# Moving three visits of the scores in the first layer, and splitting three norm sums into fp32r halves, in a two-layer decoder step

## The chip, the cores and the metric

The kernel runs on one core of one Trainium2 chip. The metric is the time of one execution in microseconds of device time; the time before is the median of three runs. The engines are named as in the profile: PE (TensorE, its weight loads shown apart as PEld), DVE (VectorE), ACT (ScalarE), POOL (GpSimd) and SP (SyncE, which issues nearly all DMAs). A profile is one further execution, taken by the hardware profiler.

## What is computed

One inference step of a decoder with two layers, for a prompt of 256 positions and for 8 samples of one position each. All 264 columns share the weights. Cut to what matters here:

```python
def rmsnorm(x, g):
    y = xf * lax.rsqrt(jnp.mean(xf * xf, axis=-1, keepdims=True) + EPS)
    return (y * g).astype(x.dtype)

# layer 0: block-sparse attention (A) beside a gated MLP (B)
q, k, v, bu, bv = jnp.split(rmsnorm(x, norm_g) @ w_in, ...)
a = moba_attention(rope(q), rope(k), v)          # softmax over causal scores
bvn = layer_norm(gelu(bv), sgu_gain)
b_out = gelu(bu) * (tril(sgu_w) @ bvn + sgu_b)
x = x + concat(a, b_out) @ w_out
# ConvFFN of each layer
h = rmsnorm(x, norm_g)
g = h @ w_gate
gc = sum(conv_w[i] * g_all[:, i:i + T] for i in range(CONV_W)) + conv_b
x = x + (gelu(gc) * (h @ w_up)) @ w_down
# layer 1: stick-breaking attention beside causal pooling, then a second ConvFFN
```

The model width is 1024, the ConvFFN's 2816, there are 8 heads of 64 in A. Everything is float32. The outputs are the new activations (after a final norm) and the new cache rows and states.

## The kernel before

Activations lie transposed: 128 features on the partitions, 264 columns (256 prompt, 8 samples) along the free axis, so the width of 1024 is 8 tiles.

**Weights and products.** The weights of all phases stream through in one order, as blocks of 128x128. Eight blocks are a tile. For each tile ACT rounds the raw weights to fp32r (wh, line 299) and DVE subtracts to get the rest (wl, line 300). An activation operand is kept as two halves as well, and a block is three PE products of 264 columns (high by high, high by low, low by high) that add into one PSUM bank; all of PE's matmuls have line 215. `split` prepares tiles three ahead; four buffers each for wh and wl mean that tile t+4 can be rounded when PE is done with tile t. The projection's outputs take turns in four PSUM banks (pool "mm"); four other banks (pool "at") serve attention and norms. Other line numbers below are those of the instruction's call.

**The phases** are in0 (160 blocks: bv, q, k, bu, v), out0 (64), ff0 and dn0 (the ConvFFN's gate and up projections, and its down projection), then in1, out1, ff1, dn1.

**Order by hand.** In in0, out0, in1 and out1 PE's instructions stay in the order in which the program gives them. Other work is hung into this order by hooks: `blk(b, f)` calls f after b blocks of the phase. SP's loads are kept in order too (`late`). All else, and PE in the ConvFFNs, is ordered by the compiler's list scheduler, which simulates the engines; DVE, ACT and POOL then run their queues in order.

**The first layer's hooks that matter here.** In in0, four visits `s_qk(t)` compute the causal scores of heads 2t and 2t+1: two mask products, eight products of q by k (S), then in `s_soft` four maxima on DVE (lines 703, 704), four exponentials on ACT (706, 707), reciprocals (708) and scalings (709 on DVE, 710 on ACT). Visit t needs q's and k's tile t with their rotation, done by `in0_evac` in four DVE steps (shuffle 670, products 672 or 674 and 675, sum 676); k's tile t is complete after block 72 + 8t. `s_tr` transposes the probabilities of one head (pt). `gm_mean` at block 100 adds bv's four tiles in three DVE steps (bsum, lines 785 to 787), the first of which is kept behind the DVE step given just before it; `gm_var` at block 108 has PE sum them over the partitions (pmu).

**The norms.** `residual` builds, for each of the 8 output tiles of out0, dn0, out1 and dn1, the new X (DVE, line 581), the next operand's halves (ACT 384, DVE 385), and a square (ACT 397) that POOL adds to an accumulator (409). `Norm.finish` calls `rstd_of`, which sums over the partitions by a PE product with a matrix of ones in fp32 (ns; each such product shows as two PE instructions), and makes R = 1/rms in two ACT steps (421, 422). The norm ahead of the first ConvFFN is f0, that ahead of layer 1 is n1, that ahead of the second ConvFFN f1; the first (n0) and the last (fin) add a second part. After f0 and f1, `gelu_set` loads another activation table behind R (517), and the evacuation of each gate tile multiplies by R (wk, line 552), followed by the convolution (553 to 556), gelu (558), the product with the up tile (563) and the split of the result (a_h 432, a_l 433). `norm1` calls finish for n1 at block 12 of in1, where PE's order is kept.

Of the kernel before, what the change touches and what calls it, by code (L numbers as in the profile page):

```python
# [9 lines left out]
F32 = mybir.dt.float32  # L10
F32R = mybir.dt.float32r
BF16 = mybir.dt.bfloat16
I32 = mybir.dt.int32
AF = mybir.ActivationFunctionType
ALU = mybir.AluOpType
# [3 lines left out]
P = 128  # L19
D = 1024  # L20
# [3 lines left out]
T = SEQ + NS  # L24
# [178 lines left out]
def tile_decoder_step(ctx: ExitStack, tc: tile.TileContext, a):  # L203
    nc = tc.nc
    v, s, g = nc.vector, nc.scalar, nc.gpsimd
# [14 lines left out]
    pe = TensorE()  # L220

    con = ctx.enter_context(tc.tile_pool(name="con", bufs=1))
# [4 lines left out]
    sm = ctx.enter_context(tc.tile_pool(name="sm", bufs=3))  # L227
# [27 lines left out]
    def vec(n):  # L255
        o, w = _VEC[n]
        return VEC[:, o:o + w]
# [117 lines left out]
    ident = cst("ident")  # L375
    ones = con.tile([P, P], F32, name="ones")
    v.memset(ones, 1.0)
    epst = con.tile([P, 1], F32, name="epst")
    v.memset(epst, EPS)

# [9 lines left out]
    class Norm:  # L390
# [17 lines left out]
            else:  # L408
                g.tensor_tensor(self.acc, self.acc, q, ALU.add)

        def finish(self, pin=False):
            return rstd_of([self.acc] + self.last, 1.0 / D, self.name, pin)

    def rstd_of(parts, scale, name, pin=False, bank=None):
        p = (bank or at)(f"ns_{name}")
        for i, x in enumerate(parts):
            mm = pe.matmul(p[:, :T], ones, x, start=i == 0, stop=i == len(parts) - 1)
            if pin:
                tc.keep_in_program_order(mm)
        R = sm.tile([P, T], F32, tag="R", name=f"R_{name}", bufs=2)  # L420
        s.activation(R, p[:, :T], AF.Ln, bias=epst, scale=scale)
        last[0] = s.activation(R, R, AF.Exp, scale=-0.5)
        return R

# [91 lines left out]
    def gelu_set():  # L516
        tc.keep_in_program_order(s.preload_act_table_set("gelu_apprx_tanh_and_others"))

    def sigmoid_set():
        tc.keep_in_program_order(s.preload_act_table_set("sigmoid_and_others"))  # L520
# [17 lines left out]

    def ffn(l, xg, R, down_evac, hooks=None):
        cw, cb = vec("cw"), vec("cb")  # L540
        wc = lambda i, j: cw[:, (l * 3 + i) * NF + j:(l * 3 + i) * NF + j + 1]
        cvo = sm.tile([P, NF, 10], F32, tag="cvo", name=f"cvo{l}", bufs=1)
        act = [mv(f"a{l}_{i}") for i in range((NF + 3) // 4)]
        half = {}

        def evac(m, o):
            n, j = m
            if n == "g":
                wk = f4(f"wk{l}_{j}", (P, 2, T))
                C = wk[:, 0, :]  # L550
                G = wk[:, 1, :]
                v.tensor_tensor(G, o, R, ALU.mult)  # L552
                s.activation(C, G, AF.Identity, scale=wc(2, j), bias=cb[:, l * NF + j:l * NF + j + 1])
                v.scalar_tensor_tensor(C[:, 1:SEQ], G[:, 0:SEQ - 1], wc(1, j), C[:, 1:SEQ], ALU.mult, ALU.add)
                v.scalar_tensor_tensor(C[:, 2:SEQ], G[:, 0:SEQ - 2], wc(0, j), C[:, 2:SEQ], ALU.mult, ALU.add)
                v.tensor_tensor(C[:, SEQ:T], C[:, SEQ:T], C0[:, l, j, :], ALU.add)
                s.activation(cvo[:, j, :], G[:, SEQ - 2:T], AF.Copy)
                s.activation(C, C, AF.Gelu_apprx_tanh)
                half[j] = wk
            else:  # L560
                wk = half.pop(j)
                C, A = wk[:, 0, :], wk[:, 1, :]
                v.tensor_tensor(A, o, C, ALU.mult)
                halves(*hl(act, j), A)

        run(orders[f"ff{l}"], lambda m, k: hl(xg, k), evac)
        nc.sync.dma_start(a[f"cv{l}"], cvo)
        lnexp()
        run(orders[f"dn{l}"], lambda m, k: hl(act, k), down_evac, hooks)

    def residual(gain, name, operand=True, R=None):
        xg = [mv(f"xg_{name}{i}") for i in range(2)] if operand else None
        nrm = Norm(name, not operand)

        def evac(m, o):
            m = m[1]
            if R is not None:
                z = sm.tile([P, T], F32, tag="rz", name=f"z_{name}{m}", bufs=4)
                v.tensor_tensor(z, o, R, ALU.mult)
                o = z  # L580
            v.tensor_tensor(X[:, m, :], X[:, m, :], o, ALU.add)
            if operand:
                operand_tile(xg[m // 4], m, X[:, m, :], gain[:, m:m + 1])
            nrm.add(m)
            if not operand:
                s.activation(X[:, m, :], X[:, m, :], AF.Copy, scale=gain[:, m:m + 1])
        return xg, nrm, evac
# [9 lines left out]
    nrm = Norm("n0", True)  # L597
# [212 lines left out]
    def gm_norm():  # L810
        Rb = rstd_of([st0["acc"]], 1.0 / 512, "sgu", bank=mmb)
        for t in range(4):
            v.scalar_tensor_tensor(bv4[:, t, :], bv4[:, t, :], vec("sg")[:, t:t + 1], Rb, ALU.mult, ALU.mult)
        bvn = sm.tile([P, 4, NS], F32, tag="bvn", name="bvn", bufs=1)
        g.tensor_copy(bvn, bv4[:, :, SEQ:T])
        nc.sync.dma_start(a["bvn"], bvn)
        st0["vgt"] = f4("vgt", (P, 2, 512))
# [45 lines left out]
    blk(40, masks)  # L863
    blk(44, gm_first)
    blk(72, sm_q)
    for t, b in enumerate((82, 95, 108, 121)):
        blk(b, s_qk, t)
    for t, b in enumerate((103, 116, 129, 142)):
        blk(b, s_tr, 2 * t)
        blk(b, s_tr, 2 * t + 1)  # L870
    blk(96, sgu_load)
# [33 lines left out]
    xg, nrm, evac = residual(vec("f0"), "f0")  # L905
    run(orders["out0"], pick([catA, catB]), evac, hk)
    fixed[0] = False
    R = nrm.finish()
    gelu_set()
    xg1, nrm1, evac = residual(vec("n1"), "n1", R=R)  # L910
    ktiles, kload = page_list(a["kt1"], "K1")
# [19 lines left out]

    def norm1():
        nonlocal R
        R = nrm1.finish()
        sigmoid_set()

    edge = f4("edge", (P, 384))
# [117 lines left out]
    fixed[0] = True  # L1055
    blk = lambda b, f, *x: hk.at(b / 8 - 1, f, *x)
    blk(12, norm1)
    blk(33, pool_sum)
    for n in range(8):
# [25 lines left out]
    xg, nrm, evac = residual(vec("f1"), "f1")  # L1085
    run(orders["out1"], pick([catA, catB]), evac, hk)
    fixed[0] = False
    R = nrm.finish()
    gelu_set()
    _, nrm, evac = residual(vec("fin"), "fin", operand=False, R=R)  # L1090
    ffn(1, xg, R, evac)
    R = nrm.finish()
    for i, (m, e) in enumerate(YD):
        x = X[:, m:e, :]
# [71 lines left out]
```

## Time and profile before

| what | value |
|---|---|
| median of 3 runs | 603.81 us (603.23 to 604.2) |
| the profiled execution | 605.38 us, span 603.6 us |
| mean granted PE clock | 0.997 |
| PE busy | 590.4 us in 4900 matmuls |
| DVE busy | 424.7 us in 745 instructions |
| ACT busy | 339.9 us in 597 |
| POOL busy | 42.8 us in 59 |
| read from and written to memory | 117.65 MB and 3.96 MB |

A row of a timeline gives an instruction's start and its duration in us, then engine, line, operation, output and inputs, and in brackets how long the engine had been idle before and what released it. A row of the chain gives start, length and what held the chain. Matmuls overlap in the pipeline, so a PE instruction's shown duration is longer than its share of the stream. A row of waits reads: who waited, for whom, us in total, how often, longest.

### The profile page before, as it was taken

The numbers are of one execution on the slowest core, as the hardware profiler recorded it, in microseconds if no ns is written. First come the engines' busy times: TensorE is split into PE (matmuls) and PEld (weight loads), VectorE is DVE, ScalarE is ACT, GpSimd is POOL, SyncE is SP. The second block draws the span as 40 slices with busy tenths as digits, with TensorE's granted clock in tenths as the row PEclk, the third lists the DMA queues.
The fourth block names the chain that finished last, engine by engine and source line by source line (L and its number), as shares of the span: only waits on it lengthen the run. The fifth ranks groups of instructions, "written<-read, shape, count | busy, mean of one in ns | idle before, by whom it ended". The sixth has DMA issues, their size and how long they took to land.

```text
span 603.6 us, 12258 instructions
## 1 busy us (share of the span) xinstructions
PE 590.4 (98%) x4900; PEld 571.4 (95%) x4900; DVE 424.7 (70%) x745; ACT 339.9 (56%) x597; POOL 42.8 (7%) x59
## 2 busy tenths in 40 slices
PE   8989999999999999999999999999999999999994
PEld 7988879999999999999999878999999999999993
DVE  6899565958878778576569676686877777755542
ACT  7557754656555656454454466656665555555431
POOL 4101002300000000001120000030000000001210
PEclk9999999999999999999999999999999999999998
DMA  8998845454554645796466763554545545455402
GB/s 310 352 378 328 272 153 205 155 204 149 201 176 174 208 150 201 260 370 212 151 251 248 262 206 113 173 205 148 208 149 201 179 171 207 152 208 171 179 1 72
DMA packets 28090, 122.39 MB, mean 203 GB/s; under 512 B 3330, under 2 KB 5250, under 8 KB 16642
## 3 DMA queue, kind: packets, MB, share of 16 engines
q1 hardware_dynamic: 27200, 120.42, 56.4%
q10 hardware_dynamic: 834, 1.20, 0.6%
q8 instruction: 38, 0.62, 0.4%
q14 instruction: 18, 0.15, 0.1%
HBM read 117.65 MB, written 3.96 MB: 201 GB/s over the span
## 4 chain that ended last, share of the span: by engine, by line
PE 91%; DVE 2%; DMA 2%; SPq 2%; ACT 2%; issue 1%; ACTq 0%; DVEq 0%
PE mm L215 83%; DMA raw<-in_w 1%; PE pv_l L215 1%; PE sc L215 1%; SPq L340 1%; PE pav L215 1%; PE pt L218 1%; DVE wl L300 1%; DMA PT<-in_pt 1%; ACT wh L299 1%; PE S L215 1%; PE Z L215 1%; SPq L274 0%; PE pf L215 0%; DVE X L1095 0%
## 5 line engine op out<-in xcount | busy, mean ns | idle before, releaser
L299 ACT ACTIVATE wh<-raw 128x1024 fp32r<-128x1024 f32 x179 | 189.6, 1062 | 198.6 <-PE mm L215 185.1
L300 DVE TENSOR_TENSOR wl<-raw,wh 128x1024 fp32r<-128x1024 f32 x179 | 219.1, 1225 | 112.5 <-ACT wh L299 111.5
L215 PE MATMUL mm<-xg_f_h,wh 128*128 128x264 f32 x704 | 200.6, 285 | 0.3 <-DVE wk L552 0.3
L215 PE MATMUL mm<-xg_f_l,wh 128*128 128x264 f32 x704 | 199.9, 284 | 0.0
L215 PE MATMUL mm<-xg_f_h,wl 128*128 128x264 f32 x704 | 198.6, 282 | 0.0
L215 PEld LDWEIGHTS mm<-xg_f_h,wh 128*128 128x128 f32 x704 | 132.2, 188 | 0.8 <-issue 0.7
L215 PEld LDWEIGHTS mm<-xg_f_l,wh 128*128 128x128 f32 x704 | 132.3, 188 | 0.1
L215 PEld LDWEIGHTS mm<-xg_f_h,wl 128*128 128x128 f32 x704 | 132.2, 188 | 0.0
L215 PE MATMUL mm<-a_h,wh 128*128 128x264 f32 x352 | 99.9, 284 | 0.0
L215 PE MATMUL mm<-a_l,wh 128*128 128x264 f32 x352 | 99.8, 284 | 0.0
L215 PE MATMUL mm<-a_h,wl 128*128 128x264 f32 x352 | 99.3, 282 | 0.0
L215 PEld LDWEIGHTS mm<-a_l,wh 128*128 128x128 f32 x352 | 66.1, 188 | 0.0
L215 PEld LDWEIGHTS mm<-a_h,wh 128*128 128x128 f32 x352 | 66.1, 188 | 0.0
L215 PEld LDWEIGHTS mm<-a_h,wl 128*128 128x128 f32 x352 | 66.1, 188 | 0.0
L215 PE MATMUL mm<-xg_h,wh 128*128 128x264 f32 x160 | 48.2, 302 | 1.1 <-ACT xg_h L384 1.1
L215 PE MATMUL mm<-xg_l,wh 128*128 128x264 f32 x160 | 46.2, 289 | 0.0
L215 PE MATMUL mm<-xg_h,wl 128*128 128x264 f32 x160 | 46.1, 288 | 0.0
L215 PE MATMUL mm<-xg_n_h,wh 128*128 128x264 f32 x128 | 38.6, 302 | 0.0
L215 PE MATMUL mm<-xg_n_l,wh 128*128 128x264 f32 x128 | 36.3, 283 | 0.0
L215 PE MATMUL mm<-xg_n_h,wl 128*128 128x264 f32 x128 | 36.2, 283 | 0.0
L215 PEld LDWEIGHTS mm<-xg_h,wh 128*128 128x128 f32 x160 | 30.8, 193 | 4.4 <-issue 2.7
L215 PEld LDWEIGHTS mm<-xg_l,wh 128*128 128x128 f32 x160 | 30.8, 193 | 0.3 <-DVE xg_l L385 0.2
(237 smaller groups left out, 842.4 us busy)
## 6 DMA issues: line engine op xcount, KB each, us to landing
raw<-in_w SPq DMA_DIRECT2D x89, 1024.0 KB, 4.8
K<-in_kt SPq DMA_DIRECT2D x32, 256.0 KB, 6.5
V<-in_vp SPq DMA_DIRECT2D x32, 256.0 KB, 5.6
raw<-in_w SPq DMA_DIRECT2D x4, 512.0 KB, 5.9
X<-in_x SPq DMA_DIRECT2D x4, 264.0 KB, 7.8
xw<-in_xw SPq DMA_DIRECT2D x2, 388.0 KB, 5.4
out_k<-k SPq DMA_DIRECT2D x1, 528.0 KB
out_v<-v SPq DMA_DIRECT2D x1, 528.0 KB, 4.9
```

The source lines that it names most:

```text
L215: return self.keep(nc.tensor.matmul(*x, **k))
L218: return self.keep(nc.tensor.transpose(*x, **k))
L299: s.activation(h, src, AF.Copy)
L300: v.tensor_tensor(l, src, h.bitcast(F32), ALU.subtract)
L340: regs.append(nc.sync.value_load(PT[0:1, i:i + 1], min_val=0, max_val=NPHYS - 1))
```

## The change

Two edits. In in0 the score visits 0, 1 and 2 move from blocks 82, 95 and 108 to 90, 98 and 109, and the first two transposes from 103 to 106. And the sums of the norms f0, n1 and f1 are taken as two products: ACT rounds the accumulator to fp32r (h), POOL subtracts to get the rest (l), and PE multiplies each with a matrix of ones in fp32r, adding both in the same bank. The ones in fp32r are a new constant, copied by POOL.

```diff
     ones = con.tile([P, P], F32, name="ones")
     v.memset(ones, 1.0)
+    onesr = con.tile([P, P], F32R, name="onesr")
+    g.tensor_copy(onesr, ones)
...
-        def finish(self, pin=False):
-            return rstd_of([self.acc] + self.last, 1.0 / D, self.name, pin)
-
-    def rstd_of(parts, scale, name, pin=False, bank=None):
+        def finish(self, pin=False, cut=False):
+            if not cut:
+                return rstd_of([self.acc] + self.last, 1.0 / D, self.name, pin)
+            h, l = [sm.tile([P, T], F32R, tag=f"acc{x}", name=f"acc{x}_{self.name}", bufs=1) for x in "hl"]
+            s.activation(h, self.acc, AF.Copy)
+            g.tensor_tensor(l, self.acc, h.bitcast(F32), ALU.subtract)
+            return rstd_of([h, l], 1.0 / D, self.name, pin, w=onesr)
+
+    def rstd_of(parts, scale, name, pin=False, bank=None, w=None):
         p = (bank or at)(f"ns_{name}")
         for i, x in enumerate(parts):
-            mm = pe.matmul(p[:, :T], ones, x, start=i == 0, stop=i == len(parts) - 1)
+            mm = pe.matmul(p[:, :T], ones if w is None else w, x, start=i == 0, stop=i == len(parts) - 1)
...
-    for t, b in enumerate((82, 95, 108, 121)):
+    for t, b in enumerate((90, 98, 109, 121)):
         blk(b, s_qk, t)
-    for t, b in enumerate((103, 116, 129, 142)):
+    for t, b in enumerate((106, 116, 129, 142)):
         blk(b, s_tr, 2 * t)
...
-    R = nrm.finish()
+    R = nrm.finish(cut=True)
     gelu_set()
...
-        R = nrm1.finish()
+        R = nrm1.finish(cut=True)
         sigmoid_set()
...
-    R = nrm.finish()
+    R = nrm.finish(cut=True)
     gelu_set()
     _, nrm, evac = residual(vec("fin"), "fin", operand=False, R=R)
```

## The prediction

> **What bounds the kernel now.** I read the page first, then PE's waits, the chain that ended last, and finally the timelines of VectorE (DVE), ScalarE (ACT) and GpSimd (POOL) around each place that the change touches.
>
> ```profile
> PE 590.4 (98%) x4900; PEld 571.4 (95%) x4900; DVE 424.7 (70%) x745; ACT 339.9 (56%) x597; POOL 42.8 (7%) x59
> ...
> PE 91%; DVE 2%; DMA 2%; SPq 2%; ACT 2%; issue 1%; ACTq 0%; DVEq 0%
> ```
>
> PE is busy for 98% of the span and carries 91% of the chain. So only two things can change the time: work taken from PE's stream, or a wait of PE inside it. The list of PE's waits has these two rows that concern us:
>
> ```profile
> PE S L215 <- DVE k L676: 2.0, 1, 2.0
> ...
> PE mm L215 <- DVE wk L552: 0.3, 2, 0.2
> ```
>
> The first row is one wait of 2.0 us: the first visit of the scores (S) stands in PE's queue before the rotated k is there. The second is one short wait at the start of each ConvFFN. The windows around the first wait show which engine it comes from (the columns are stretch, length, then busy time of PE, weight loads, DVE, ACT, POOL, then clock, DMA share and GB/s):
>
> ```profile
> 31.00:42.00 11.00, 8.96 (x75) 8.30 (x74) 10.03 (x22) 5.53 (x7) 0.00 (x0) 1.00 0.99 370
> 42.00:54.00 12.00, 12.00 (x101) 10.85 (x100) 11.68 (x40) 8.76 (x25) 0.13 (x1) 1.00 1.02 386
> ```
>
> DVE is busy for 11.68 of 12.00 us from 42 to 54, directly behind the wait. This is the fact that my forecast rests on: in this stretch DVE has a backlog, and PE is saved from it only because it lost 2 us first. The DMA engines are full too (0.99 and 1.02), but the visits issue no DMA and the change moves no load past another in SP's queue; a weight that came late would show as a wait of PE on wl, and there is none in the list now.
>
> **The moved visits.** These rows are PE's stream here, from the timeline and then from the chain:
>
> ```profile
> 40.49 0.93 PE L215 MATMUL S<-k,q 64*128 64x128 f32 x8 [2.04 <-DVE k L676]
> ```
>
> ```profile
> 41.42 4.92 PE mm L215 x39
> 46.34 1.09 PE S L215 x10
> ...
> 50.54 0.65 PE pt L218 x6
> ...
> 53.02 1.09 PE S L215 x10
> 54.10 0.64 PE pmu L215 x2
> ...
> 134.98 178.98 PE mm L215 x1476
> ```
>
> One projection product takes 178.98 / 1476 = 0.121 us, a block of three 0.364 us. Moving the first visit from block 82 to 90 puts 8 blocks, 2.9 us, in front of it. PE would then issue its products at 40.49 - 2.04 + 2.91 = 41.36. They could start at 40.49 in this trace, so k is there and the 2.04 us are gone. The second visit (95 to 98) comes at 46.34 - 2.04 + 3 x 0.364 = 45.4, and the first transposes (pt, 103 to 106) at 50.54 - 2.04 + 1.09 = 49.6. What the two wait for:
>
> ```profile
> 43.58 0.43 DVE L676 TENSOR_TENSOR k<-k,rz_k 128x264 f32<-128x264 f32 x1
> ```
>
> ```profile
> 45.83 0.90 ACT L710 ACTIVATE p<-p,st 128x256 f32<-128x256 f32 x2
> ```
>
> The second k ends at 44.01, before 45.4. The probabilities of the first visit end at 46.73; with the visit 0.87 us later and DVE no faster, they still come before 49.6. So neither becomes a new wait by itself.
>
> What is late next is pmu, the product that sums bv for the gating's mean. It stays at block 108, while the third visit moves from in front of it (108) to behind it (109). PE without any wait reaches pmu at 54.10 - 2.04 - 1.09 = 50.97. It needs bsum, three additions on DVE, and everything of gm_var, the third visit and the stream is queued behind it on PE. From DVE's timeline:
>
> ```profile
> 42.52 0.29 DVE L703 TENSOR_REDUCE st<-S 128x1 f32<-128x128 f32 x1
> ...
> 49.56 1.22 DVE L300 TENSOR_TENSOR wl<-raw,wh 128x1024 fp32r<-128x1024 f32 x1
> 50.70 0.43 DVE L785 TENSOR_TENSOR bsum<-bv 128x264 f32<-128x264 f32 x1
> 51.04 0.43 DVE L676 TENSOR_TENSOR k<-k,rz_k 128x264 f32<-128x264 f32 x1
> ...
> 51.66 0.42 DVE L786 TENSOR_TENSOR bsum<-bsum,bv 128x264 f32<-128x264 f32 x1
> ...
> 52.09 0.42 DVE L678 TENSOR_TENSOR bu<-mm,R_n 128x264 f32<-128x264 f32 x1
> ...
> 53.36 0.43 DVE L787 TENSOR_TENSOR bsum<-bsum,bv 128x264 f32<-128x264 f32 x1
> 53.70 1.22 DVE L300 TENSOR_TENSOR wl<-raw,wh 128x1024 fp32r<-128x1024 f32 x1
> ```
>
> bsum ends at 53.79, which was just in time for 54.10. Since DVE had no idle time, an earlier PE does not make it earlier; only another order of DVE's queue does, and the compiler chooses that order anew. One addition occupies the queue for 51.04 - 50.70 = 0.34 us. From the start of the first to that of the third lie 2.66 us, of which 2 x 0.34 are bsum; the other 1.98 us are steps that bsum does not need (bu, masks, scalings, the last k). With all of them behind it, bsum ends at 53.79 - 1.98 = 51.81. With the second visit's four maxima behind it as well (43.58 - 42.52 = 1.06 us in the first visit) it ends at 50.75, and PE does not wait. With the order as it is it ends at 53.79. With the next weight split in front of it (50.70 - 49.56 = 1.14 us; its tile is consumed earlier now, so it is ready earlier) it ends at 54.93. I take 52.0: the bsum steps stand earlier in the program than most of the filling, but some of it slips in between dependent additions, as it does now. I allow 0.2 us from the end of bsum to pmu (in this trace at most 0.31, from 53.79 to 54.10). The wait is 52.0 + 0.2 - 50.97 = 1.2 us. The stage gains 2.04 - 1.2 = **0.8 us**; between the ends, from 2.0 gained to 2.1 lost. Behind pmu PE has slack against DVE, so nothing more is lost or won.
>
> **The two norms ahead of the ConvFFNs (f0, f1).** The sum over partitions is two fp32 instructions now:
>
> ```profile
> 122.01 0.45 PE ns_f L215 x2
> ...
> 313.96 0.45 PE ns_n L215 x2
> ```
>
> It becomes two fp32r products of the shape of the stream's own, 2 x 0.121 = 0.24 us: 0.21 us less on PE for each of three norms. For that, h (ACT) and l (POOL) stand between the accumulated squares and the product. These rows price them, POOL's first:
>
> ```profile
> 118.76 1.01 POOL L409 TENSOR_TENSOR acc_f<-acc_f,sq_f 128x264 f32<-128x264 f32 x1 [1.89 <-ACT sq_f L397]
> ```
>
> ```profile
> 587.61 0.76 POOL L409 TENSOR_TENSOR acc_fin<-acc_fin,sq_fin 128x264 f32<-128x264 f32 x1 [5.28 <-ACT sq_fin L397]
> ```
>
> ```profile
> 119.75 1.06 ACT L299 ACTIVATE wh<-raw 128x1024 fp32r<-128x1024 f32 x1 [1.13 <-PE mm L215]
> ...
> 123.45 1.28 ACT L517 ACT_TABLE_LOAD   x1
> ...
> 132.79 0.41 ACT L432 ACTIVATE a_h<-wk 128x264 fp32r<-128x264 f32 x1
> ```
>
> The squares are summed at 119.77. ACT is held by wh until 120.81, so h ends at 121.2 and l, at 1.01, at 122.3. The product is not pinned here, stood at 122.01 and can slide behind other blocks, so PE need not wait; R comes 0.3 to 3 us later. R's successors are the table load and the first gate's chain, at whose end this row stands:
>
> ```profile
> 134.41 0.77 DVE L552 TENSOR_TENSOR wk<-mm,R_f 128x264 f32<-128x264 f32 x2
> ```
>
> It frees the banks for which PE waits 0.15 us on average (0.3 for two). A later R loses little, because ACT and DVE do a weight split meanwhile that now stands in the chain behind R; a wh less in it (1.06) covers a delay of that size. I count the 0.15 as gone: 2 x (0.21 + 0.15) = **0.72 us gained**. If that cover fails, one wh more in the chain costs 1.06 us in each.
>
> **The norm ahead of layer 1 (n1).** Here the product is pinned at block 12 of the projection, so PE waits for l if it is late.
>
> ```profile
> 311.55 0.96 POOL L409 TENSOR_TENSOR acc_n<-acc_n,sq_n 128x264 f32<-128x264 f32 x1 [3.70 <-ACT sq_n L397]
> ```
>
> ```profile
> 312.47 1.06 ACT L299 ACTIVATE wh<-raw 128x1024 fp32r<-128x1024 f32 x1 [1.06 <-issue]
> ```
>
> ```profile
> 117.94 1.23 DVE L300 TENSOR_TENSOR wl<-raw,wh 128x1024 fp32r<-128x1024 f32 x1 [0.43 <-ACT wh L299]
> ...
> 313.56 1.23 DVE L300 TENSOR_TENSOR wl<-raw,wh 128x1024 fp32r<-128x1024 f32 x1 [0.76 <-ACT wh L299]
> ```
>
> The squares are summed at 312.51, with wh already on ACT until 313.53. h ends at 313.94, l starts at 313.97, under DVE's wl, which runs until 314.79. POOL's addition at 118.76 started with 0.41 us of a wl (117.94 to 119.17) left and took 0.25 more than the lone one of 0.76. By that ratio 0.82 us left cost 0.50: l takes 1.26 and ends at 315.23, and the second product ends at about 315.4, against 314.41 now: **1.0 us lost**. With a bare 0.76 it is 0.5 lost; if the compiler puts h ahead of wh, l is in time and the 0.21 is won.
>
> [...]
>
> The copy of the ones to fp32r is one POOL step near the start, on an engine that is busy 7% of the span, and its first reader comes at 122; uncovered it would cost about one addition, 0.8 us.
>
> **The sum.** -0.8 - 0.72 + 1.0 = -0.5 us. The profiled execution took 605.38 us for a span of 603.6, that is 1.57 over the median of 603.81; the difference applies to either, so 604.9 for that execution and 603.3 for the median.
>
> **The rivals.** The bound for a difference is 0.2%, 1.2 us.
>
> - *PE meets no wait at pmu* (bsum by 50.8, its fillers and the second maxima behind it). For it: these steps are free to move. Against: they stand in front in this trace. Then -2.0 - 0.72 + 1.0 = -1.7, 602.1; with h ahead of wh as well -2.0 - 0.72 - 0.21 = -2.9, 600.9.
> - *Slower: DVE's order stays.* pmu then waits for 53.79 and the third visit, now behind it, comes on top: 53.79 + 0.2 - 50.97 - 2.04 = 1.0 lost, with the norms +1.3, 605.1; with a weight split in front, 2.4 and 606.2. The stage turns from gain to loss when bsum ends after 52.8. For it: DVE is full. Against: bsum's place in the program is ahead of the filling.
> - *Slower: the late R lengthens both gate chains* by one wh each: -0.8 + 1.0 - 0.42 + 2.1 = +1.9, 605.7. For it: PE already waits there. Against: a wh leaves that chain.
>
> **How the numbers follow.** Forecast 0.48 (its own range 602.6 to 604.5), no wait at pmu 0.32, DVE's order 0.13, late R 0.07. Faster by over 0.2% is the first rival and a little of the forecast's lower tail, 0.36; slower is the last two less their mild ends, and a little of the forecast's upper tail, 0.19; within it 0.45. The range 601.2 to 605.4 takes in the first rival but its extreme, and the milder ends of the slow ones.
>
> **What would show it.** PE's waits: no S <- k, instead pmu <- bsum of about 1.2 us; and a wait of the second ns_n product on l of about 1.3 us. No wait on wk. ns chain pieces of 0.24 us. The forecast is wrong if pmu does not wait, if bsum ends after 52.8, or if the wk wait grows beyond 0.2.

## The result: slower, by a new wait at pmu and the slow clock behind it

| | kernel before | changed kernel |
|---|---|---|
| median (range) of 4 runs | 603.61 us (603.23 to 604.2) | 608.96 us (607.44 to 611.03) |
| profiled execution, span | 605.38, 603.6 | 611.03, 609.3 |
| mean granted PE clock of that execution | 0.997 | 0.990 |

The ratio is 1.0085 (95% interval 1.0068 to 1.0102): 5 us slower, where 0.5 us faster was forecast. The list of PE's waits in the changed kernel holds the answer in its first row (lines of the changed kernel are 7 higher here: bsum is 792 to 794, and GpSimd's product of the gating matrix is 788; l, which is new, is 418). Its profiled execution is the slowest of the four, so what its rows show is more than the usual loss.

```profile
PE pmu L215 <- DVE bsum L794: 3.9, 1, 3.9
...
PE ns_n L215 <- POOL accl_n L418: 1.2, 1, 1.2
```

The wait of the first visit (S on k) and the two waits on wk are gone, as forecast. In their place PE waits 3.9 us at pmu, where 1.2 was forecast. PE's timeline of the changed kernel at that place:

```profile
41.73 0.93 PE L215 MATMUL S<-k,q 64*128 64x128 f32 x8
...
45.91 0.93 PE L215 MATMUL S<-k,q 64*128 64x128 f32 x8
...
49.79 0.82 PE L218 MATMUL pt<-CST,p 128*128 128x128 f32 x6
...
51.05 0.28 PE L215 MATMUL mm<-xg_h,wl 128*128 128x264 f32 x1
55.25 1.25 PE L215 MATMUL pmu<-bsum,ones 128*128 128x264 f32 x2 [3.92 <-DVE bsum L794]
...
56.74 0.42 PE L215 MATMUL mm<-xg_h,wl 128*128 128x264 f32 x1
```

The visits and transposes came without a wait, and PE was at pmu by 51.33. Behind the wait a projection product shows 0.42 us where it showed 0.28 ahead of it, and these start 0.22 us apart instead of 0.12. The windows of the changed kernel say why (stretch, length, busy time of PE, weight loads, DVE, ACT, POOL, then clock, DMA share, GB/s):

```profile
50.00:54.00 4.00, 1.33 (x12) 1.12 (x10) 3.90 (x12) 3.14 (x9) 0.47 (x1) 1.00 1.04 400
54.00:58.00 4.00, 2.75 (x11) 2.03 (x13) 2.17 (x2) 0.39 (x1) 0.91 (x1) 0.62 0.75 306
58.00:62.00 4.00, 4.00 (x22) 3.35 (x21) 1.92 (x7) 2.71 (x6) 0.00 (x0) 0.53 0.01 4
62.00:66.00 4.00, 4.00 (x37) 3.73 (x37) 3.22 (x9) 2.91 (x8) 0.00 (x0) 1.00 0.36 113
```

The granted clock is 0.62 and 0.53 from 54 to 62, behind the wait: 22 matmuls in 4 us, where the next row has 37. In the kernel before, the same stretches are at full clock:

```profile
54.00:58.00 4.00, 4.00 (x33) 3.90 (x32) 4.00 (x11) 2.90 (x10) 2.08 (x1) 1.00 0.85 290
58.00:62.00 4.00, 4.00 (x35) 3.40 (x34) 3.80 (x7) 3.58 (x7) 0.00 (x0) 1.00 0.30 121
```

DVE's timeline of the changed kernel shows why bsum was late, and POOL's what held its third addition:

```profile
49.10 1.22 DVE L300 TENSOR_TENSOR wl<-raw,wh 128x1024 fp32r<-128x1024 f32 x1
50.23 0.28 DVE L710 TENSOR_REDUCE st<-S 128x1 f32<-128x128 f32 x1
50.43 0.42 DVE L711 TENSOR_REDUCE st<-S 128x1 f32<-128x256 f32 x1
50.76 0.16 DVE L715 RECIPROCAL st<-st 128x2 f32<-128x2 f32 x1
50.84 0.41 DVE L685 TENSOR_TENSOR bu<-mm,R_n 128x264 f32<-128x264 f32 x1
51.17 0.28 DVE L716 TENSOR_SCALAR p<-p,st 128x128 f32<-128x128 f32 x1
51.36 1.22 DVE L300 TENSOR_TENSOR wl<-raw,wh 128x1024 fp32r<-128x1024 f32 x1
52.49 0.16 DVE L715 RECIPROCAL st<-st 128x2 f32<-128x2 f32 x1
52.69 0.29 DVE L716 TENSOR_SCALAR p<-p,st 128x128 f32<-128x128 f32 x1
52.89 0.43 DVE L792 TENSOR_TENSOR bsum<-bv 128x264 f32<-128x264 f32 x1
53.35 0.43 DVE L793 TENSOR_TENSOR bsum<-bsum,bv 128x264 f32<-128x264 f32 x1
53.82 1.38 DVE L794 TENSOR_TENSOR bsum<-bsum,bv 128x264 f32<-128x264 f32 x1
```

```profile
53.53 1.38 POOL L788 TENSOR_TENSOR sguc<-sguc,tril 128x512 f32<-128x512 f32 x1 [36.88 <-ACT p L717]
...
125.79 0.76 POOL L418 TENSOR_TENSOR accl_f<-acc_f,acch_f 128x264 fp32r<-128x264 f32 x1 [0.54 <-ACT acch_f L417]
...
318.79 1.47 POOL L418 TENSOR_TENSOR accl_n<-acc_n,acch_n 128x264 fp32r<-128x264 f32 x1 [1.41 <-ACT acch_n L417]
```

All three additions stand behind two weight splits and the whole softmax of the second visit; in the kernel before they stood one by one between such steps, and ahead of the second split. The program says why: the first addition is kept behind the DVE step given just before it. With the second visit at block 95, that step is the weight split given behind block 96; with the visit at 98 and the additions at 100, it is the visit's last scaling (L716, at 52.69). In every profile here with the visit at 95, the first addition follows directly on a weight split, and in every one with the visit at 98 and the additions at 100 directly on that scaling. The third addition took 1.38 us instead of 0.43, under GpSimd's product.

### The profile page after: what moved, and what is told of

Its sections match the earlier page's. It is cut to its first block, busy times and chain, and to the rows that moved or that the text cites. A ratio compares the mean times of both kernels' runs of the same rounds, so it can differ in the third digit from the quotient of the medians.

```text
span 609.3 us, 12269 instructions
## 1 busy us (share of the span) xinstructions
PE 593.5 (97%) x4900; PEld 574.1 (94%) x4900; DVE 426.8 (70%) x745; ACT 342.3 (56%) x600; POOL 45.1 (7%) x63
## 4 chain that ended last, share of the span: by engine, by line
PE 89%; DVE 5%; DMA 2%; issue 1%; ACT 1%; SPq 1%; POOL 0%; ACTq 0%; DVEq 0%
PE mm L215 82%; DVE wl L300 2%; DMA raw<-in_w 1%; PE pv_l L215 1%; PE sc L215 1%; PE pav L215 1%; DMA PT<-in_pt 1%; PE pt L218 1%; SPq L340 1%; PE Z L215 1%; PE S L215 1%; ACT wh L299 0%; PE pf L215 0%; DVE X L1102 0%; PE pm L215 0%
## 5 line engine op out<-in xcount | busy, mean ns | idle before, releaser
L215 PE MATMUL mm<-xg_h,wh 128*128 128x264 f32 x160 | 49.7, 311 | 1.0 <-ACT xg_h L386 1.0
```

The lines of the kernel that those rows point to most:

```text
L215: return self.keep(nc.tensor.matmul(*x, **k))
```

## The experiments

The leading theory (A) was that the stage of the visits makes the whole loss; the rival (B) that the norms' halves make a good part of it. Ratios are to the kernel before on the same chip, with 95% intervals. "First pav" is where the chain enters the products with V, the first point behind the whole stage; it stood at 93.58 in the profile of before.

**The two halves of the change, each alone.** e1_visits has the moved visits with the norms as before; e2_norms has the norms, with this edit to the changed kernel:

```diff
-    for t, b in enumerate((90, 98, 109, 121)):
+    for t, b in enumerate((82, 95, 108, 121)):
...
-    for t, b in enumerate((106, 116, 129, 142)):
+    for t, b in enumerate((103, 116, 129, 142)):
```

> Only the three visits and the first transposes are moved; the norms are as before. Theory A (the stage of the visits makes the whole loss: DVE's order puts two weight splits and the second visit's softmax ahead of bsum, PE waits about 3.9 us for it, and PE's clock is halved for some 6 us behind that wait): 4.5 to 6 us slower than before, 608.5 to 609.5, a wait on bsum of 3 to 4 us and a granted clock near 0.99. Rival B (the norm halves make a good part of it, since the order of every queue is chosen anew): at most 3 us slower.

> Only the three norm sums are taken as halves; the visits stay at 82, 95, 108. From the profile of the changed kernel: f0 and f1 gain 0.3 to 0.6 us each, n1 loses 1.1 by a wait of PE on l of 1.2 us, so theory A expects 603.4 to 604.1, no difference that can be measured. Rival B: 2 us or more slower.

Measured: the visits alone 608.98 us, 1.0083 [1.0070, 1.0096]; the norms alone 604.29, 1.0002 [0.9993, 1.0011]. The moved visits make the whole loss; B falls. The chain reaches the first pav here:

```profile
99.06 2.80 PE pav L215 x32
```

```profile
92.05 2.80 PE pav L215 x32
```

The first row is the changed kernel, the second e2_norms: 7.0 us, of which 3.92 are the wait and the other 3.1 fall where the clock is low. (The two profiled executions, 611.03 and 604.03, lie as far apart; the medians differ by 5.) In e1_visits the wait was 3.14 and the first pav came at 96.19. e2_norms showed no wait at the first visit either, though its visits are those of before. That raised the question of how large the removed wait is at all.

**The kernel before, profiled again** (three more profiles, no edit).

> The kernel before once more, for a second profile of it. Theory A (the 2.0 us wait of the first visit for k belongs to the one execution that was profiled, which took 605.38 against a median of 603.81, and is smaller in the usual one): a profiled time near 603.6 to 604.1, a wait S <- k of 0 to 0.6 us, the product pmu at 52.5 to 53.0 us. Rival (every execution has the wait, and the move removed 2 us): the wait is 1.7 us or more again and pmu stands near 54.

> The kernel before, a third profile. Theory A as for the second one, which missed (it had the wait of 2.0 us again, and 605.29): since timed runs of that kernel have a median of 604.1 and the kernels with unmoved visits showed no such wait in their profiles, I now expect the wait to come and go with the issue of the cache loads on SP around 19 to 23 us: four issues in under 3.3 us, no wait at the visit, time near 604; in over 3.7 us, a wait of 2 us, time near 605.3. Rival: the wait is there whatever those issues take, and the timed runs have it too.

> The kernel before, a fourth profile; the same as for the third one: four issues of the cache loads on SP in under 3.3 us, no wait at the first visit and a time near 604; in over 3.7 us, a wait of 2 us and a time near 605.3. Rival: the wait is there whatever the issues take.

Measured: 605.29, 603.91 and 604.61 us. Their waits of the first visit, one profile after the other:

```profile
PE S L215 <- DVE k L676: 2.0, 1, 2.0
```

```profile
PE S L215 <- DVE k L676: 0.7, 1, 0.7
```

```profile
PE S L215 <- DVE k L676: 1.1, 1, 1.1
```

The first of them speaks against theory A, and alone it would have spoken for a constant wait; the other two show that its size varies. With the profile of before the waits are 2.04, 1.99, 0.72 and 1.10, and time less wait is 603.34, 603.30, 603.19 and 603.51: nearly all of the spread of these four executions is this wait. Against about 603.3, the medians of this kernel, 603.6 to 604.3 over the runs, hold some 0.3 to 1.0 us of it; this is an estimate, since it takes the other executions to differ by this wait alone. It goes in part with SP's four issues of the cache (K), which the next raw weights stand behind. They read so in the profile of before and in b_again2:

```profile
18.77 3.91 SPq L274 DMA_DIRECT2D K<-in_kt  x4
22.73 0.66 SPq L274 DMA_DIRECT2D raw<-in_w  x1
```

```profile
18.83 2.66 SPq L274 DMA_DIRECT2D K<-in_kt  x4
21.54 0.43 SPq L274 DMA_DIRECT2D raw<-in_w  x1
```

The raw weights were issued 1.2 us later where the wait was longer (rounding to wh began at 26.16 and 24.71). These issues are not the only cause: in b_again3 they took 2.52 us and the wait was still 1.1, and in e2_norms they took 2.60 and there was no wait. The expectation of none below 3.3 us was too sharp, and what sets the size of the wait stays open.

**The clock.** e4_warm and e11_warm40 put idle products in front of pmu, so that PE waits without being idle:

```diff
+        for i in range(24):
+            pe.matmul(pmu[:, :256], warm[:, :P], warm, start=i == 0, stop=i == 23)
```

> The changed kernel, with 24 more products of 128x256 bf16 on PE in front of pmu; they need nothing from DVE and their sums are overwritten by pmu, so they take about 2.6 us of the time in which PE would stand idle for bsum. If the idle stretch itself throws the clock (theory A's second half), the remaining idle time of 1.3 us does not, and the kernel gets faster by about 3 us although it does more work: 605.5 to 606.5, clock 0.997. If the clock has nothing to do with it, 609 or a little more.

> The changed kernel with 40 idle bf16 products of 128x256 in front of pmu instead of the 24 of the earlier run: 4.4 us by the 2.65 us that those 24 took, more than the longest wait for bsum seen with this order and an undisturbed GpSimd. Theory A2 (the clock falls because PE idles for over 3 us, and about half of the loss is that clock): clock 0.995 to 0.997 in all timed runs, no wait on bsum, the first product with V at 96 to 96.5 us and the time 608.0 to 608.8 with all runs within 1.5 us of each other, though PE stands at pmu for longer than in the changed kernel. Rival (the clock falls for another reason, such as the power of the stage): some runs with 0.990 to 0.993 again, spread over 3 us, median 609 or more.

Measured: with 24, 607.48 us, 1.0069 [1.0051, 1.0088]; its profiled run took 606.73 at a clock of 1.00 in all windows from 50 to 62, but two of its six runs took 609.7 and 610.24 at a mean clock of 0.993: 24 presumably did not always cover the wait, and the median came out 1 us over the expectation. With 40, 607.98, 1.0063 [1.0050, 1.0076], and all five runs within 0.31 us. The mean clock of these five still reads 0.993 to 0.997, so that figure alone doesn't separate them. In its timeline:

```profile
50.92 4.54 PE L215 MATMUL pmu<-warm 128*128 128x256 bf16 x40
55.30 0.61 PE L215 MATMUL pmu<-bsum,ones 128*128 128x264 f32 x2
```

PE stood 4.4 us at pmu doing nothing useful, longer than the 3.9 us that it idled in the changed kernel, and the kernel was 1 us faster by the medians, though the intervals of the two ratios overlap. The profiles show it more sharply, in the stretch from the start of pmu to the first pav, which holds the same work in every kernel with the third visit behind pmu. It takes 40.7 us in e11_warm40 and 40.8 in e4_warm, both without idling, and 43.8 in the changed kernel. In e1_visits pmu starts where it starts in e4_warm (53.85 and 53.86), but behind 3.14 us of idling:

```profile
96.19 2.80 PE pav L215 x32
```

```profile
94.67 2.80 PE pav L215 x32
```

The first row is e1_visits, 1.5 us later at the same work, at a clock of 0.68 and 0.89 from 54 to 62 instead of 1.00. So here the idling cost more than its length.

**GpSimd's product.** e5_mul125 hung the product's instruction at block 125; e10_sgu112 moved the load, the mask and the product from block 96 to 112.

```diff
-    blk(96, sgu_load)
+    blk(112, sgu_load)
```

> The changed kernel, with GpSimd's product of the gating weights by the triangle moved from block 96 to block 125. In the changed kernel it starts at 53.53 and DVE's third bsum addition, which takes 0.43 alone, takes 1.38 and ends just behind it. If GpSimd holds that addition up, it falls back to 0.43 here, the wait on bsum to about 3.0 us, and the time by 0.95 us if the clock is still thrown (608.0), by up to 4 us (605) if a wait of 3.0 us is too short to throw it. If the addition is slow for another reason, nothing changes.

> The changed kernel with the gating matrix's load, its mask on DVE and its product on GpSimd hung at block 112 instead of 96, so that the product starts some 5 us later. Theory A1 (the third addition of bsum is held up by GpSimd's product, which costs about 1 us of the wait and its share of the slow clock): the third addition takes 0.43 us, bsum ends at 53.6 to 54.3, PE's wait for it falls from 3.9 to 2.4 to 3.1 us, and the time to 607 to 608.3. Rival (the addition was slow for another reason, or the product is a by-stander): 1.3 us again and 608.6 to 609.4.

Measured: in e5_mul125 the product did not move away, since it still started when its data landed, now 0.06 us ahead of the third addition: 610.04 us, 1.0092 [1.0078, 1.0107], wait 5.0. But it repeats the pairing. Its addition, and then its product:

```profile
54.35 1.49 DVE L797 TENSOR_TENSOR bsum<-bsum,bv 128x264 f32<-128x264 f32 x1
```

```profile
54.29 1.26 POOL L791 TENSOR_TENSOR sguc<-sguc,tril 128x512 f32<-128x512 f32 x1 [37.54 <-DMA sguc<-in_sguw]
```

The first of the additions that DVE starts after that product's start ends 0.28 to 0.29 us behind the product: the third addition at 55.20 against 54.91 (changed kernel) and 55.84 against 55.55 (here), the second one at 54.58 against 54.30 in e11_warm40. Where the product started only after the addition, as in e1_visits (53.37, product 53.84), the addition took 0.43. What couples the two steps is not shown. With the product out of the way, e10_sgu112 took 607.28 us, 1.0046 [1.0033, 1.0059]: third addition 0.43, wait 1.9 (below the expected 2.4: against e1_visits PE came 0.7 us later, at 51.45 instead of 50.71, and the additions ended 0.5 us earlier, at 53.31 instead of 53.80). Yet its clock fell:

```profile
54.00:58.00 4.00, 4.00 (x23) 3.09 (x22) 2.41 (x5) 2.28 (x6) 0.00 (x0) 0.62 0.64 251
```

Its first pav is at 95.73, 3.7 us behind e2_norms: 1.9 of wait and most of the rest of clock, since pmu to pav took 42.4 us against 40.7.

**Which of the three visits.** e13_third108 and e14_second95 undo one visit's move in the changed kernel (109 to 108, 98 to 95); e9_first_only moves the first visit alone in the kernel before (82 to 90).

> The changed kernel with the third visit at block 108, in front of pmu as before, instead of 109. Theory A4 (the 1.09 us of the third visit used to lie in front of pmu and cover DVE; the change took that cover away): PE's wait for bsum falls by about 1.1 us to 2.0 to 2.9, the clock falls less or not at all behind it, and the time is 606 to 607.7. Rival (the third visit's own place does not matter, because the compiler's order of DVE shifts along with it): wait over 3 us and 608.5 or more.

> The changed kernel with the second visit back at block 95 and all else as changed. In the compiled program DVE's order is then: weight split, first addition of bsum, second, next weight split, third addition; in the changed kernel all three stand behind both weight splits and behind the second visit's softmax. Theory A8 (the second visit's three blocks are what sends bsum behind its softmax): bsum ends 1 to 2 us earlier than in the changed kernel, PE's wait falls from 3.9 to 1.0 to 2.3 us, and the time to 604.5 to 606.5, the rest being the one weight split that stays in front. Rival (the first visit or the third one's place behind pmu makes the loss): 607.5 or more.

> The kernel before with the first visit alone moved from block 82 to 90; norms, other visits, transposes and pmu as before, the third visit in front of pmu. Theory A7 (what costs is that softmax steps of the first visit, done on DVE before 45 us, are pushed into the stretch before pmu and pt, where DVE has no time): PE waits 1.5 to 3 us in all at pt or pmu, and the time is 605 to 607. Rival (the loss came from the third visit's place behind pmu): no wait over 0.6 us, 603.6 to 604.4.

| | us | ratio | wait for bsum | third addition ends |
|---|---|---|---|---|
| changed | 608.96 | 1.0085 [1.0068, 1.0102] | 3.9 | 55.20 |
| third back | 608.06 | 1.0060 [1.0044, 1.0075] | 1.8 | 54.52 |
| second back | 607.87 | 1.0061 [1.0044, 1.0078] | 2.3 | 52.99 |
| first alone | 603.95 | 0.9996 [0.9987, 1.0005] | 0 | 52.27 |

The waits fell as expected, or further, but both times lie above what was expected, because the clock fell to 0.62 and 0.57 from 54 to 58 behind these shorter waits too. For e9_first_only theory A7 was wrong and its rival right: the first visit 8 blocks later makes no new wait. Its DVE order still has bsum ahead of the second weight split:

```profile
51.85 0.42 DVE L787 TENSOR_TENSOR bsum<-bsum,bv 128x264 f32<-128x264 f32 x1
52.81 1.22 DVE L300 TENSOR_TENSOR wl<-raw,wh 128x1024 fp32r<-128x1024 f32 x1
```

With the second visit at 98, as in the changed kernel and in e13_third108, the first addition is kept behind its last scaling, and all three come behind both splits; with the second at 95 but the third behind pmu, the third addition alone stays behind the second split. So either of the two later moves is enough to leave a wait of about 2 us, and with it the fall of the clock; only with both undone, and the transposes back at 103, is there none. The second visit's move alone was not run, nor was the first addition without what keeps it in place.

**Taking pmu or bsum out of the way.** e3_var115 puts pmu seven blocks later in the changed kernel; e6_mean84 gives bsum earlier; e7_mean84_best also leaves n1 uncut; e12_mean84_tr112 moves the transposes as well.

```diff
-    blk(108, gm_var)
+    blk(115, gm_var)
```

> The changed kernel with the sum of bv on PE (pmu) at block 115 instead of 108: 7 blocks, 2.55 us later, which is where the unmoved visits had it in time. Theory A6 (pmu came too early for DVE's order; its readers have slack): the wait on bsum falls from 3.9 to under 1.3 us, the clock stays at 1.00, and the time is 604.3 to 605.8. Rival (DVE's queue is late for all that follows): the wait appears at another product, and 606 or more.

> The changed kernel with the three additions of bsum given at block 84 instead of 100, so that they stand early in DVE's queue; everything else as changed. Theory A (the whole loss is the wait at pmu and the slow clock behind it): no wait of PE on bsum, clock 0.99 to 1.00 from 50 to 62 us, and the time falls to that of the kernel with the new norms alone, 0.9990 to 1.0010 of the kernel before, some 603.4 to 604.6 us. If the usual execution of before does have a wait at the first visit, the move then wins it: 602 us. Rival (the visits themselves stand badly, or the norms make a good part): 605.5 or more.

> The changed kernel with bsum at block 84 and with n1's sum as before (one fp32 product of the accumulator); f0 and f1 as two halves. By the checkpoints of the two profiles n1's halves cost 1.1 us and those of f0 and f1 gain 0.3 to 0.6 each. Theory A: 1.1 us under the kernel with bsum at 84 and all three norms cut, 0.998 to 0.999 of the kernel before, 602.6 to 603.4 us. Rival (norms count for nothing beside the noise of the loads): within 0.3 us of the kernel with all three cut.

> The kernel with bsum at block 84, n1 as before and the moved visits, and now the first two transposes at blocks 112 and 118 instead of 106 and 116. Theory A3 (the visits moved by 8 blocks but what reads their result by only 3, so DVE's full queue is late for whichever reader comes first: pmu in the changed kernel, pt with bsum early): no wait on pt nor on bsum over 0.3 us, the first product with V at 91.8 to 92.3 us, and the time that of the kernel with the visits where they were and f0 and f1 cut, 602.5 to 603.5. Rival (DVE has too little time for the stage in this order whatever the deadlines): another wait of 1.5 to 2 us in its place, at pmu, at the next transposes or on a weight split, and 604.5 to 605.5.

Measured: e3_var115 604.13 us, 1.0001 [0.9992, 1.0010], no wait, clock 1.00. Its DVE order is that of the changed kernel, its third addition even under GpSimd's product (0.99 us, ending at 55.05), but PE comes only then:

```profile
55.68 0.61 PE L215 MATMUL pmu<-bsum,ones 128*128 128x264 f32 x2
```

One number takes the whole loss away: readers of pmu had slack, pmu itself had none. With bsum early instead, e6_mean84 took 605.46, 1.0019 [1.0002, 1.0036], and e7_mean84_best 604.9, 1.0020 [1.0008, 1.0031]: no wait at pmu, but a new one at the transposes, with the clock still 1.00 in the profiles. Both took longer than expected.

```profile
PE pt L218 <- DVE st L715: 1.8, 1, 1.8
```

The 1.1 us that n1 uncut was to win do not show in these ratios. They do in the profiles: from the first pav to that of layer 1, e6_mean84 took 285.57 us and e7_mean84_best 284.16. But five of the eleven runs of e7_mean84_best took 605.96 to 606.74 at a mean clock of 0.992 or 0.993, the other six 603.46 to 604.9 at 0.995 or 0.996, so the clock probably fell in some executions of one and the same kernel; none of those was profiled.

With later transposes too, e12_mean84_tr112 took 604.74, 1.0008 [0.9997, 1.0018], and its rival was right: the wait went on to the next ones.

```profile
PE pt L218 <- ACT p L714: 0.9, 1, 0.9
PE S L215 <- ACT pT L727: 0.7, 1, 0.7
```

**The parts that do no harm.** e8_f_only has f0 and f1 as two halves, with visits and n1 as before; e15_first_f adds the first visit at 90.

> The visits where they were before, f0 and f1 as two halves, n1 as before. Theory A: the same gain of 0.7 to 1.2 us from f0 and f1, 0.998 to 0.9990 of the kernel before, 602.6 to 603.4 us, no wait on wk; equal to the kernel with bsum at 84 and the moved visits, because the move itself gains nothing in a usual execution. Rival (the move gains 2 us once pmu does not wait): 1.5 to 2 us slower than that kernel.

> The parts that did no harm together: the first visit alone at block 90, and f0 and f1 as two halves; the other visits, the transposes, pmu and n1 as in the kernel before. Theory A (the first visit's wait of 0.7 to 2.0 us in the profiles is taken away without a new one, and the two norms win 0.4 to 0.6 each): no wait at S, pmu or wk, 602.4 to 603.2 us, 0.9970 to 0.9985 of the kernel before. Rival (the first visit's move wins nothing): the same as with the two norms alone, 0.9982, 603.0 or more.

Measured: e8_f_only 603.14 us, 0.9982 [0.9973, 0.9991]; e15_first_f 602.68, 0.9972 [0.9962, 0.9982]. Both beat both kernels. The first visit's move is worth another 0.6 us by these ratios, within what the wait was estimated to be, though the intervals overlap. In the kernel before, the same move (e9_first_only) won 0.2 us, with an interval from 0.3 lost to 0.8 won.

## Why the prediction was wrong, step by step

**"The 2.04 us are gone": right, but mis-sized.** The wait vanished, but 2.04 was its size in an execution 1.57 us above the median. The difference to the median was then carried over to either kernel unchanged; by the four profiles it was the wait itself. In a usual execution 0.3 to 1.0 us were to be won by the estimate above, and the one run of this move alone won 0.2. PE also came to the moved visit later than forecast, at 41.73 instead of 41.36, and to pmu at 51.33 instead of 50.97; why is not shown.

**"I take 52.0" for the end of bsum: the step that failed.** It was argued from bsum's place in the program, ahead of most of the filling. But the second visit stands at block 98, ahead of bsum at 100, and the first addition is kept behind the DVE step given just before it. The move made that step the visit's last scaling instead of a weight split, so the whole softmax of the visit, with both splits between its steps, came ahead of all three additions, which without hindrance end at 53.80 (e1_visits). The forecast even had the visit's maxima behind bsum as a case. The forecast's own worst case, with a weight split in front, had 54.93; the changed kernel passed even that, at 55.20, because GpSimd's product held the third addition for 0.95 us. The row that showed such stretching, of a step of POOL beside one of DVE (the addition at 118.76 in the kernel before: 1.01 us, with 0.41 us of a weight split left, against 0.76 alone), was used for the norm and not here.

**A wait was priced at its length: a missing term.** "DVE's order stays" was the right rival, at 606.2 with the split in front. The rest came from the clock, where the forecast had "nothing more is lost or won" behind pmu. Against the 40.7 to 40.8 us from pmu to the first pav in e4_warm, e11_warm40, e6_mean84 and e7_mean84_best, where the clock stayed at 1.00, the changed kernel took 43.8, some 3.1 us more. Four others took 42.3 to 42.4, some 1.6 more, behind waits of 1.92 (e10_sgu112), 2.25 (e14_second95), 3.14 (e1_visits) and 5.0 us (e5_mul125). In e13_third108, with the third visit in front of pmu and a wait of 1.82, the stretch took 41.1 against 39.5 in e8_f_only. So in these runs what the clock cost did not grow with the wait. Nor did the clock fall only behind idling of over 3 us, as theory A2 of e11_warm40 had it: it was 0.62 and 0.57 from 54 to 58 behind the waits of 1.82, 1.92 and 2.25 us too, with PE busy for 1.75 to 2.76 of the 4 us before. And it stayed at 1.00 with waits of 2.04 (before), 1.8 (e6_mean84) and 2.1 (e7_mean84_best). What sets these apart isn't shown.

**The norms: right in sum, each larger.** f0 and f1 were to win 0.72 together; e8_f_only won 1.1 (0.0018 of 604.1, interval 0.5 to 1.6). The wait on wk went, and no other came in its place, so the later R did not lengthen the gate chain. The profiles agree: from the first pav to that of layer 1, a stretch with f0 in it, the four of the kernel before took 284.75 to 284.77 us and e8_f_only 284.15; from there to the end, with f1, they took 225.2 and 224.6. For n1, l was put at 1.26 us and took 1.47, from 318.79, beside a weight split of DVE from 318.43 to 319.66; the l of f0, with no step of DVE beside it, took 0.76. PE waited 1.16 at the second product. By the ratios of e2_norms and e8_f_only, 0.0020, n1's cut costs 1.2 us, and by the same stretch of their profiles (285.57 against 284.15) 1.4, against 1.0 forecast:

```profile
127.81 0.29 PE L215 MATMUL ns_f<-acch_f,onesr 128*128 128x264 f32 x1
128.78 0.28 PE L215 MATMUL ns_f<-accl_f,onesr 128*128 128x264 f32 x1
...
318.76 0.39 PE L215 MATMUL ns_n<-acch_n,onesr 128*128 128x264 f32 x1
320.31 0.39 PE L215 MATMUL ns_n<-accl_n,onesr 128*128 128x264 f32 x1 [1.16 <-POOL accl_n L418]
```

At f0 the products stand unpinned, 1 us apart, and the stream runs between them; at n1 PE's order is kept and it waits.

## What to carry to other kernels

A wait in one profiled execution is worth its size there only if that execution is a usual one: if its time lies above the median by about the wait, look at a second profile before moving work. When work moves past a product that an engine with no idle time feeds, ask for the compiled order of that engine's queue. If a step there is kept behind the one given before it, look which step that will be after the move, and move the waiting product along with the work. In this kernel a wait of PE of 1.8 us or more could cost 1.6 to 3.1 us beside its own length, and did not always.

## What the runs showed of the hardware that was not expected

PE's granted clock fell to 0.57 to 0.62 for 4 us after waits of 1.8, 1.9 and 2.3 us (e13_third108, e10_sgu112, e14_second95), and stayed at 1.00 after others of 1.8 to 2.1 (e6_mean84, before, e7_mean84_best). Behind waits of 1.9, 2.25, 3.1 and 5.0 us it cost the same 1.6 us from pmu to the first pav, and behind one of 3.9 it cost 3.1. Forty idle products of 4.4 us were cheaper than 3.9 us of idling, by 1 us and with runs within 0.31 us of each other instead of 3.6. And one product on GpSimd, an engine busy for 7% of the span, made an addition of 0.43 us on DVE take 0.96 to 1.49, depending on where in the product it began; it ended 0.28 to 0.29 us behind it in all five profiles in which it began during the product.
